# Start stage of a Fourier and attention block: transform tables split earlier, final sums taken before the halves of u, squares of the latent rows asked one block ahead

## The chip, the cores and the metric

The kernel runs on one core of one Trainium2 chip. The metric is device microseconds (us) of one execution. The kernel before takes 1317.43 us, the median of three runs (1315.72 to 1318.75).

## The reference

One mixer layer over 512 latent tokens of width 2048, with 256 context tokens and one conditioning vector `c`. A combined projection of the normalised and modulated rows feeds attention (branch A) and a two-dimensional Fourier mix (branch B); both are gated, projected, merged and projected once more.

```python
shift, scale, gate = jnp.split(silu_c @ w_ada[l] + b_ada[l], 3, axis=-1)
h = _modulate(_rmsnorm(xs, norm_g[l]), shift[:, None], scale[:, None])
p = h @ w_l
...
y = jnp.fft.fftn(ug, axes=(1, 3), norm="ortho").real      # u, the columns u_b of p
...
y_b = (_fourier_mix(u_b) * jax.nn.silu(z_b)) @ w_pb       # z, the columns z_b of p
```

Everything is float32. The kernel multiplies it as three products of split numbers: each operand is written as a high part (rounded) and a low part (what is left), and high·high, low·high and high·low are summed.

## The kernel before, in words

Only the start stage, about the first 180 us, is touched by the change. The rest is eight groups of a Strassen-like scheme for the other columns of the projection, attention, the two branch projections and the output; its instructions stay in the same order on TensorE.

**Rows and tiles.** `xt` holds the 16 blocks of 128 latent channels ("rows" 0 to 15, 512 tokens each). The start stage computes eight tiles of 128 columns: t = 0 to 3 are u, t = 4 to 7 are z. It goes over the row blocks (`kb`) in order; `some(n)` issues the next n tiles of `start_work`, three matmuls each (L329 high·high, L330 with the low part of the row, L331 with the low part of the weights). The four sums of u stay in four PSUM banks (`pb`). The sums of z go through two banks (`pc`) and are added to `part` in SBUF by `keep` (L636 a copy on ACT; L640 an add on DVE; L638 the last add, with the correction `corr`).

**Two forms of a row.** The norm factor `rx` needs the squares of all 16 rows. So rows 0 to 4 (`RAWS` = 5) are multiplied as gain·x without it (`make_raw`, L611 and L612) and their sums are multiplied by `rx` later (`spread_rows`, L737). Rows from 5 on are made with it (`make_h`, L619 to L621; L620 on ACT makes the high part, L621 on DVE the low part). `squares` (L526 on ACT, L528 on DVE) adds up the squares of one chunk of `xt` as it comes; `norm_sum` (L591 to L595) sums them over partitions on TensorE, with square root and reciprocal; `norm_spread` (L600, L601) brings the factor to all partitions.

**Modulation.** `modulate(k)` (L542) is a matrix-vector product of `c` with 2 MB of `w_ada` for row block k, loaded as two transfers into four buffers; ACT copies its sum (L551), TensorE turns it (L555) and DVE makes gain and shift (L561 to L564) in `columns(k)`. Row k can be made only after that.

**Weights.** Pieces of 512 KB or less are loaded into `raw` buffers (L214) and split: ACT makes the high part (L178), DVE the low part (L179). In the first blocks SP issues the loads; from block 5 on ACT issues them (`asks[0] = nc.scalar`, `ask_more`), and from the end of the start stage SP again. From block 8 on two more raw buffers are lent (`MORE_RAW`).

**The Fourier mix.** After the last tiles, the two tables over positions (`fsq`, two pieces of 512 KB) and the table over channels (`fch`) are split, `halves(g)` forms the sum and the difference of the two halves of u's tile g (L817, L818) and splits them (`uh`, `ul`), `channels(g)` multiplies by `fch`, `positions(g)` by `fsq`, and `gate_b` (L864, L865) applies the gate of z. Then group 0 begins with the products named `x`; its weights are the pieces `R`, split as `wlo<-R`.

**What sets the order.** TensorE's order is the order of the code (a hand-written schedule). On DVE and ACT a scheduler orders the instructions; `behind(ins)` ties the instructions in its block behind the given ones. Each engine then runs its instructions strictly in order, so an instruction that waits holds all behind it.

Of the kernel before, what the change touches and what calls it, by code (L numbers as in the profile page):

```python
# [18 lines left out]
P = 128  # L19
D = 2048  # L20
T = 512
# [19 lines left out]
MORE_RAW = 8  # L41
# [80 lines left out]
def block_kernel(ctx, tc, xT, ctx_rows, ctx_toks, x, c_row, w_ss, w_gate, vecs, qkg, rope, dft_c, dft_s,  # L122
# [335 lines left out]
    mr, mrp = region("mr")  # L458
# [51 lines left out]
    csum = pap.tile([P, 256], F32, name="csum")  # L510
    sf = pap.tile([P, RAWS, 32], F32, name="sf")
    nc.vector.memset(sf, 0.0)
    corr = ppool.tile([P, NS], F32, name="corr")
    rx = pap.tile([P, T], F32, name="rx")
    t = hm_tile([P, 2, T], F32, name=uid("nm"))
    pick, root = t[:, 0, :].rearrange("p (t c) -> p t c", t=4), t[:, 1, :P]
# [6 lines left out]
    def squares(a, n):  # L523
        for q in range(a, a + n):
            v = sq[q // 2][:, q % 2, :]
            nc.scalar.activation(v, xt[:, q, :], ACT.Square)  # L526
            if q:
                nc.vector.tensor_tensor(total, total, v, op=ALU.add)  # L528

# [102 lines left out]

    def keep(t, acc, kb, nk):
# [3 lines left out]
        elif kb + nk == KK:  # L637
            nc.vector.scalar_tensor_tensor(dst, acc, corr[:, t : t + 1], dst, op0=ALU.add, op1=ALU.add)  # L638
# [43 lines left out]

    def split_next():
        split_piece(next(e for e in ahead if e.out is None and e.kind != "raw"))
# [7 lines left out]
    with tc.manual_schedule(engines={mybir.EngineType.PE}):  # L692
# [10 lines left out]
        for kb in range(RAWS):  # L703
# [29 lines left out]
        ask_more(act, 2)  # L733
# [6 lines left out]
        with behind(ins):  # L740
            spread_rows(4, 5)
            split_next()
        wada[7] = wada_load(7)
        some(2)
        modulate(6)
        some(2)
        with behind((columns(6),)):
            spread_rows(6, 7)
        some(1)
# [3 lines left out]
        some(2)  # L753
        ask_more(ins[1], 2)

        for kb in range(6, KK, 2):
            ins = make_h(kb), make_h(kb + 1)
            ins = ins[0] + ins[1]
            if kb == MORE_RAW:
# [1196 lines left out]
```

## Time and profile before

| quantity | value |
|---|---|
| median of three runs | 1317.43 us (1315.72 to 1318.75) |
| the profiled execution | 1318.22 us, its span 1316.4 us, 0.79 us above the median |
| mean granted TensorE clock | 0.992 |
| TensorE busy | 1282.3 us, 97% of the span |
| DVE busy | 1010.2 us, 77% |
| ACT busy | 691.7 us, 53% |
| data moved | 318.54 MB, 242 GB/s in the mean |

A row of the timeline reads: start, duration, engine, line, operation, tile written <- tiles read, shape, count, and in brackets the idle time of the engine just before it with what ended that idle time. "ACTq" is an issue of a transfer on ACT's queue. A row of the windows view reads: stretch, then busy us and number of instructions of TensorE (PE), its weight loads (PEld), DVE, ACT and POOL, then the granted TensorE clock (1.00 is full speed), the share of the DMA engines and GB/s. A row of the waits view reads: engine, tile, line, the thing waited for: us in total, times, longest.

### The profile page before, as it was taken

Reading aid. Unit: us, or ns where it says so; the run is one execution under the profiler, and the core shown is the slowest. Engines: PE = TensorE matmul, PEld = TensorE weight load, DVE = VectorE, ACT = ScalarE, POOL = GpSimd, SP = SyncE. Lnnn points to the kernel's source line nnn. Section 1 sums busy time; section 2 is a strip of 40 time slices with the busy share of each in tenths; the row PEclk is TensorE's granted clock in tenths of the full one; section 3 lists DMA queues with packets and bytes.
Section 4 is the critical chain, followed back from the end, with each engine's and each line's share of the span. In section 5 each row is a group of like instructions: output and inputs, shape, how many; then the busy total and the mean of one; then the engine's idle time right before and its main releaser. Section 6 shows DMA issues by size and latency. Waiting matters only on the chain.

```text
span 1316.4 us, 17688 instructions
## 1 busy us (share of the span) xinstructions
PE 1282.3 (97%) x6568; PEld 1051.8 (80%) x6568; DVE 1010.2 (77%) x1326; ACT 691.7 (53%) x1095; POOL 176.2 (13%) x236
## 2 busy tenths in 40 slices
PE   8899899999999999999999999999999999999997
PEld 5566698888888788888888888788888888888885
DVE  4677889978788688666677756688888867887676
ACT  4433555555545455434345454666667645565544
POOL 0011011020112101011012020011210212221210
PEclk9899999999999999999999999999999999999998
DMA  9899558798799989986969898658872899998985
GB/s 381 327 347 380 189 160 205 233 210 286 201 248 267 253 295 280 290 227 172 263 208 254 297 230 249 211 193 249 257 231 88 221 247 243 252 211 225 225 205 171
DMA packets 103862, 318.54 MB, mean 242 GB/s; under 512 B 9824, under 2 KB 33120, under 8 KB 99680
## 3 DMA queue, kind: packets, MB, share of 16 engines
q0 software_dynamic: 29136, 115.36, 38.0%
q1 hardware_dynamic: 50016, 172.56, 36.9%
q10 hardware_dynamic: 24624, 29.50, 6.5%
q8 instruction: 51, 0.84, 0.3%
q14 instruction: 35, 0.29, 0.1%
HBM read 283.30 MB, written 34.09 MB: 241 GB/s over the span
## 4 chain that ended last, share of the span: by engine, by line
PE 78%; DMA 6%; DVE 6%; ACT 2%; issue 2%; ACTq 0%; DVEq 0%
PE banks L329 10%; PE banks L330 10%; PE banks L331 10%; PE x L331 7%; PE x L330 7%; PE x L329 7%; PE y L330 6%; PE y L329 6%; PE y L331 6%; PE banks L1444 2%; DMA wr<-in_w_g 2%; DVE wlo L179 2%; DMA wr<-in_ctx_toks 1%; PE pd L542 1%; DMA wa<-in_w_ss 1%
## 5 line engine op out<-in xcount | busy, mean ns | idle before, releaser
L178 ACT ACTIVATE whi<-R 128x1024 fp32r<-128x1024 f32 x138 | 145.2, 1059 | 141.9 <-PE banks L331 49.5
L179 DVE TENSOR_TENSOR wlo<-R,whi 128x1024 fp32r<-128x1024 f32 x138 | 167.5, 1221 | 55.5 <-ACT whi L178 55.3
L179 DVE TENSOR_TENSOR wlo<-wr,whi 128x1024 fp32r<-128x1024 f32 (+2 forms) x124 | 148.3, 1204 | 66.0 <-ACT whi L178 65.9
L178 ACT ACTIVATE whi<-wr 128x1024 fp32r<-128x1024 f32 (+2 forms) x124 | 128.8, 1044 | 128.4 <-PE y L331 37.4
L329 PE MATMUL banks<-whi,s 128*128 128x512 f32 x396 | 157.0, 396 | 2.1 <-DVE ev L1012 1.5
L330 PE MATMUL banks<-wlo,s 128*128 128x512 f32 x396 | 155.2, 392 | 0.0
L331 PE MATMUL banks<-whi,s 128*128 128x512 f32 x396 | 155.2, 392 | 0.0
L329 PE MATMUL x<-whi,s 128*128 128x512 f32 x352 | 137.2, 390 | 0.0
L331 PE MATMUL x<-whi,s 128*128 128x512 f32 x352 | 137.0, 389 | 0.0
L330 PE MATMUL x<-wlo,s 128*128 128x512 f32 x352 | 136.9, 389 | 0.0
L330 PE MATMUL y<-wlo,s 128*128 128x512 f32 x316 | 123.1, 389 | 1.9 <-DVE wlo L179 1.9
L329 PE MATMUL y<-whi,s 128*128 128x512 f32 x316 | 123.1, 389 | 0.6 <-DVE cxe L1165 0.6
L331 PE MATMUL y<-whi,s 128*128 128x512 f32 x316 | 122.8, 389 | 0.0
L282 POOL DMA_DIRECT2D R<-in_w_g x64 | 56.0, 877 | 421.4 <-DVE wlo L179 246.7
L178 ACT ACTIVATE s<-wr 128x512 fp32r<-128x512 f32 (+2 forms) x93 | 60.5, 676 | 65.0 <-DMA wr<-cf_d 22.3
L179 DVE TENSOR_TENSOR s<-wr,s 128x512 fp32r<-128x512 f32 (+2 forms) x93 | 67.0, 749 | 32.3 <-ACT s L178 31.6
L329 PEld LDWEIGHTS banks<-whi,s 128*128 128x128 f32 x396 | 74.4, 188 | 17.6 <-ACT whi L178 1.9
L331 PEld LDWEIGHTS banks<-whi,s 128*128 128x128 f32 x396 | 74.4, 188 | 15.4
L330 PEld LDWEIGHTS banks<-wlo,s 128*128 128x128 f32 x396 | 74.5, 188 | 14.3 <-DVE wlo L179 0.4
L331 PEld LDWEIGHTS x<-whi,s 128*128 128x128 f32 x352 | 66.1, 188 | 13.8
L329 PEld LDWEIGHTS x<-whi,s 128*128 128x128 f32 x352 | 66.1, 188 | 13.7
L330 PEld LDWEIGHTS x<-wlo,s 128*128 128x128 f32 x352 | 66.1, 188 | 13.6
(305 smaller groups left out, 2860.0 us busy)
## 6 DMA issues: line engine op xcount, KB each, us to landing
wr<-in_w_g SPq DMA_DIRECT2D x128, 512.0 KB, 5.3
R<-in_w_g POOLq DMA_DIRECT2D x64, 512.0 KB, 7.7
wa<-in_w_ss POOLq DMA_DIRECT2D x18, 1024.0 KB, 8.0
R<-in_w_g SPq DMA_DIRECT2D x32, 512.0 KB, 5.7
wr<-in_w_gate SPq DMA_DIRECT2D x32, 512.0 KB, 5.1
wa<-in_w_ss SPq DMA_DIRECT2D x14, 1024.0 KB, 13.4
wr<-in_w_o SPq DMA_DIRECT2D x24, 512.0 KB, 7.7
R<-in_w_o POOLq DMA_DIRECT2D x24, 512.0 KB, 8.7
```

The costliest lines, as they stand in the source:

```text
L178: first = nc.scalar.activation(hi, src, ACT.Copy)
L179: return first, nc.vector.tensor_tensor(lo, src, hi.bitcast(F32), op=ALU.subtract)
L282: nc.gpsimd.dma_start(chain[e.pc], e.nxt, accum_op=ALU.add)
L329: nc.tensor.matmul(o, ah, bh, start=start, stop=False, skip_group_check=cont)
L330: nc.tensor.matmul(o, ah, bl, start=False, stop=False, skip_group_check=cont)
L331: nc.tensor.matmul(o, al, bh, start=False, stop=stop, skip_group_check=cont)
L542: nc.tensor.matmul(acc[32 * j : 32 * j + 32], c2[:, n, :], w[:, k, :], start=n < 4, stop=n >= KK - 4)
L1444: nc.tensor.transpose(tp[:, k * P : (k + 1) * P], p[:, k * P : (k + 1) * P], ident)
```

## The change

1. The first table over positions and the table over channels are loaded one piece earlier and split inside block 10; the second table is split after the start stage. `fsq` becomes two tiles. `fch` and the first `fsq` lie in a pool that lives longer.
2. The two extra raw buffers are gone; instead a raw buffer counts as free as soon as its piece is split.
3. The halves of u are tied behind z's last keeps: halves 0 and 1 behind the keep of tile 4, halves 2 and 3 behind that of tile 5. The weights of group 0 are split one by one behind z's last keep and the positions of each group.
4. The squares of a chunk are asked one block earlier (chunks 1 and 2 in block 0, then one chunk each), and the last chunk's are asked ahead of the split and the row of block 4. The norm's sum moves behind the sums of shifts and the mat-vec of block 4, its spreading one tile later, and the mat-vec for row 6 into block 4.
5. Two loads of weights at the end of block 4 are issued by SP, where ACT issued them.
6. In block 10 the mat-vecs of rows 12 and 13 no longer follow each other directly.

The core of the diff:

```diff
     for p in start_pieces():
-        if p[2:5:2] == (KK - 4, 4):
-            for q in range(2):
-                stream(("dfts", q), dft_s[:, q], 1024, 2, "raw")
+        if p[2:5:2] == (KK - 4, 0):
+            stream(("dfts", 0), dft_s[:, 0], 1024, 2, "raw")
             stream(("dftc", 0), dft_c, 256, 1, "raw")
+        elif p[2:5:2] == (KK - 4, 4):
+            stream(("dfts", 1), dft_s[:, 1], 1024, 2, "raw")
...
     def split_next():
-        split_piece(next(e for e in ahead if e.out is None and e.kind != "raw"))
+        e = next(e for e in ahead if e.out is None and e.kind != "raw")
+        split_piece(e)
+        if e.key[1][2] >= RAWS:
+            e.raws = []
...
             some(5 if kb == 0 else 2)
+            shift_sums(kb)
+            copied = modulate(kb + 1)
             if kb == RAWS - 1:
                 norm_sum()
-            shift_sums(kb)
-            copied = modulate(kb + 1)
             some(1 if kb == 0 else 2)
-            with behind((copied, columns(kb + 1))):
+            last = columns(kb + 1)
+            if kb + 2 == RAWS:
+                with behind((copied,)):
+                    copied = squares(*XCH[RAWS])
+            with behind((copied, last)):
                 if kb:
                     split_next()
             if kb + 1 < RAWS:
-                ins = make_raw(kb + 1)
+                with behind((copied,)):
+                    ins = make_raw(kb + 1)
                 some(2 if kb == 0 else 4)
                 with behind(ins):
-                    squares(*XCH[kb + 1])
-                    if kb + 2 == RAWS:
-                        squares(*XCH[RAWS])
+                    for i in ((1, 2), (3,), (4,), ())[kb]:
+                        squares(*XCH[i])
             else:
-                some(1)
-                act = norm_spread()
-                some(3)
-            if kb + 2 <= RAWS:
+                some(2)
+                norm_spread()
+                modulate(6)
+                some(2)
+            for _ in range(1 if kb + 2 <= RAWS else 2):
                 load_start()
         shift_columns()
         asks[0] = nc.scalar
-        ask_more(act, 2)
...
+            elif kb == 10:
+                some(4)
+                modulate(12)
+                some(2)
+                columns(12)
+                some(2)
+                modulate(13)
+                some(1)
+                columns(13)
+                some(1)
+                with behind(ins):
+                    split_table(0)
+                    split_from(get(("dftc", 0)), fch[:, 0, :], fch[:, 1, :])
             else:
                 some(8 if kb == 8 else 4)
                 modulate(kb + 2)
...
-    for q in range(2):
-        split_from(get(("dfts", q)).rearrange("p (m n) -> p m n", m=2), fsq[:, 0, q], fsq[:, 1, q])
-    raw = get(("dftc", 0))
-    split_from(raw, fch[:, 0, :], fch[:, 1, :])
-    for g in range(4):
-        halves(g)
     ordered = ExitStack()
     ordered.enter_context(tc.manual_schedule(engines={mybir.EngineType.PE}))
+    for n in range(4):
+        next(work)
+        if n < 2:
+            with behind((finals[-1],)):
+                halves(2 * n)
+                halves(2 * n + 1)
     for _ in work:
         pass
...
         positions(g)
         if g < 2:
             channels(g + 2)
+        with behind((finals[-1],)):
+            for e in ahead[:g]:
+                split_piece(e)
     ordered.close()
+    look[0] = 4
```

Line numbers in the rows of the change are those of the changed kernel: most start-stage lines stand one to three lines off (L178 is its split on DVE, L177 on ACT, L328 to L330 its three products, L641 its last keep, L643 its keep).

**ACT, from block 3 to block 4.** `ado` is the copy of a mat-vec's sum, `L526` the squares, `whi_513` (in the change `whi_523`) the high part of block 4's weights, `s_517` (`s_527`) the high part of row 4. Before:

```order
33 L551 COPY ado_496<-pd_159 128x256
34 L611 ACTIVATE s_517<-xt,gain 128x512
35 L566 COPY sf<-shift 128x1
36 L178 ACTIVATE whi_513<-wr_460 128x1024
37 L526 ACTIVATE s_156<-xt 128x512 x2
38 L526 ACTIVATE s_157<-xt 128x512 x2
39 L526 ACTIVATE s_158<-xt 128x512 x2
40 L636 COPY part<-pb_224 128x512
```

Now:

```order
33 L552 COPY ado_500<-pd_157 128x256
34 L526 ACTIVATE s_154<-xt 128x512 x2
35 L526 ACTIVATE s_155<-xt 128x512
36 L567 COPY sf<-shift 128x1
37 L526 ACTIVATE s_155<-xt 128x512
38 L526 ACTIVATE s_156<-xt 128x512 x2
39 L177 ACTIVATE whi_523<-wr_464 128x1024
40 L612 ACTIVATE s_527<-xt,gain 128x512
```

The last six squares stood behind row 4 and the split of block 4's weights; now they stand ahead of both.

**TensorE, block 4.** `pb` and `pc` are the first two tiles of block 4, L591 (L592) the norm's sum over partitions, L575 (L576) the sums of shifts, L542 (L543) the mat-vec for row 5. Before:

```order
122 L329 MATMUL pc_559<-s_517,whi_513 128x512
123 L330 MATMUL pc_559<-s_518,whi_513 128x512
124 L331 MATMUL pc_559<-s_517,wlo_514 128x512
125 L591 MATMUL pc_564<-s_151,ones 128x512
126 L575 MATMUL pd_159<-wr_460,sf 32x256 x4
127 L542 MATMUL pd_160<-wa_463,c_131 32x256 x8
128 L542 MATMUL pd_160<-wa_465,c_131 32x256 x8
```

Now:

```order
122 L328 MATMUL pc_557<-s_527,whi_523 128x512
123 L329 MATMUL pc_557<-s_528,whi_523 128x512
124 L330 MATMUL pc_557<-s_527,wlo_524 128x512
125 L576 MATMUL pd_157<-wr_464,sf 32x256 x4
126 L543 MATMUL pd_158<-wa_467,c_128 32x256 x8
127 L543 MATMUL pd_158<-wa_469,c_128 32x256 x8
128 L592 MATMUL pc_585<-s_149,ones 128x512
```

The norm's sum has moved behind twenty small matmuls.

**DVE, the end of the start stage.** `u`, `ul` are halves of u and their low parts, `part<-pc` z's last keeps. Before, ahead of these rows, stand the splits of both `fsq` pieces and of `fch`:

```order
194 L817 TENSOR_TENSOR u_1366<-part 128x256
195 L818 TENSOR_TENSOR u_1366<-part 128x256
196 L817 TENSOR_TENSOR u_1371<-part 128x256
197 L818 TENSOR_TENSOR u_1371<-part 128x256
198 L179 TENSOR_TENSOR wlo_1391<-R_1343,whi_1390 128x1024
199 L179 TENSOR_TENSOR ul<-u_1366,uh 128x512
200 L179 TENSOR_TENSOR ul<-u_1371,uh 128x512
201 L817 TENSOR_TENSOR u_1376<-part 128x256
202 L818 TENSOR_TENSOR u_1376<-part 128x256
203 L817 TENSOR_TENSOR u_1381<-part 128x256
204 L818 TENSOR_TENSOR u_1381<-part 128x256
205 L638 SCALAR_TENSOR_TENSOR part<-pc_1394,corr,part 128x512
```

Now:

```order
192 L641 SCALAR_TENSOR_TENSOR part<-pb_225,corr,part 128x512
193 L178 TENSOR_TENSOR fsq_1353<-wr_1161,fsq_1353 128x1024
194 L641 SCALAR_TENSOR_TENSOR part<-pc_1366,corr,part 128x512
195 L837 TENSOR_TENSOR u_1380<-part 128x256
196 L838 TENSOR_TENSOR u_1380<-part 128x256
197 L837 TENSOR_TENSOR u_1385<-part 128x256
198 L838 TENSOR_TENSOR u_1385<-part 128x256
199 L641 SCALAR_TENSOR_TENSOR part<-pc_1390,corr,part 128x512
```

z's first last keep stood behind three tables, all halves of u and a split of `R`; now it stands behind one table.

More of the change, by code (lines that the diff above doesn't have):

```diff
@@ L38 @@
 NS = len(START)
-MORE_RAW = 8
 RAWS = 5
@@ L513, in block_kernel @@
     corr = ppool.tile([P, NS], F32, name="corr")
+    fch = ppool.tile([P, 2, 256], F32R, name="fch")
+    fsq = [ppool.tile([P, 2, 2, T], F32R, name="fsq0")]
     rx = pap.tile([P, T], F32, name="rx")
     t = hm_tile([P, 2, T], F32, name=uid("nm"))
-    pick, root = t[:, 0, :].rearrange("p (t c) -> p t c", t=4), t[:, 1, :P]
+    pick, root, csum = t[:, 0, :].rearrange("p (t c) -> p t c", t=4), t[:, 1, :P], t[:, 1, 256:]
     nc.gpsimd.memset(pick, 0.0)
@@ L752, in block_kernel @@
         columns(7)
-        some(2)
-        ask_more(ins[1], 2)
+        some(3)
         for kb in range(6, KK, 2):
@@ L810, in block_kernel @@
     ul = fnp.tile([P, 4, T], F32R, name="ul")
-    fch = fnp.tile([P, 2, 256], F32R, name="fch")
-    fsq = fnp.tile([P, 2, 2, 2, T], F32R, name="fsq")
+    fsq.append(fnp.tile([P, 2, 2, T], F32R, name="fsq1"))
+    split_table(1)
     def halves(g):
```

25 lines of the change are left out of this document (11 added, 14 removed).

## The prediction

> **What bounds the kernel now.** First the share of busy time: TensorE works 97% of the span, so what can be won is what TensorE waits, and what it does at half its clock. The waits view lists TensorE's waits over the whole span; these are the four that the change can reach:
>
> ```profile
> PE pc L329 <- DVE part L638: 4.9, 1, 4.9
> PE pc L591 <- DVE s L528: 4.6, 1, 4.6
> PE pd L542 <- DMA wa<-in_w_ss: 2.7, 2, 1.8
> PE pb L329 <- ACT s L620: 1.8, 1, 1.8
> ```
>
> All lie in the first 160 us. The windows view shows where, and where the granted clock falls:
>
> ```profile
> 50.00:60.00 10.00, 4.91 (x27) 1.98 (x30) 6.27 (x10) 4.37 (x10) 0.00 (x0) 0.66 0.61 250
> 70.00:80.00 10.00, 10.00 (x86) 5.84 (x86) 5.88 (x12) 2.43 (x4) 2.16 (x4) 0.83 0.86 316
> 110.00:120.00 10.00, 8.37 (x72) 5.43 (x70) 8.81 (x17) 3.90 (x6) 1.62 (x3) 1.00 0.98 382
> 150.00:160.00 10.00, 5.08 (x17) 3.78 (x16) 10.00 (x18) 6.14 (x9) 0.00 (x0) 0.83 0.79 304
> 190.00:200.00 10.00, 10.00 (x46) 8.28 (x45) 10.00 (x13) 5.68 (x6) 3.41 (x4) 1.00 1.01 200
> ```
>
> In all but the last of these TensorE lacks time or clock; after 160 us it is full. I call the four places A (50 to 60), B (69 to 75), D (118 to 121) and E (150 to 160), and go through them on the axis of the profiled execution.
>
> **A, the norm's sum.** TensorE's timeline at A, then the same two small products one block earlier, at full clock; DVE's adds of squares; on ACT the copy of a mat-vec's sum in block 1 and in block 3, and the squares of block 3:
>
> ```profile
> 56.41 2.08 PE L591 MATMUL pc<-s,ones 128*128 128x512 f32 x2 [4.57 <-DVE s L528]
> 58.41 1.08 PE L575 MATMUL pd<-wr,sf 128*32 128x256 f32 x8
> 59.27 2.17 PE L542 MATMUL pd<-wa,c 128*32 128x256 f32 x32
> ```
> ```profile
> 42.44 0.64 PE L575 MATMUL pd<-wr,sf 128*32 128x256 f32 x8
> 42.90 1.91 PE L542 MATMUL pd<-wa,c 128*32 128x256 f32 x32
> ```
> ```profile
> 52.49 3.87 DVE L528 TENSOR_TENSOR s<-s,s 128x512 f32<-128x512 f32 x5
> ```
> ```profile
> 26.57 0.37 ACT L551 COPY ado<-pd 128x256 f32<-128x256 f32 x1 [2.78 <-PE pd L542]
> 44.93 0.38 ACT L551 COPY ado<-pd 128x256 f32<-128x256 f32 x1 [3.36 <-PE pd L542]
> 49.24 3.22 ACT L526 ACTIVATE s<-xt 128x512 f32<-128x512 f32 x6
> ```
>
> Before, two tiles of block 4 run, begun some 2.4 us before the wait, at 49.4; then the sum waits 4.57 us for five adds (3.87). The change removes that wait, but puts the six squares (3.22) ahead of the split and the row of block 4, and their adds too. So the first tile of block 4 now waits. Two steps fix its start. First, in block 1 the copy of the mat-vec's sum, at 26.57, falls behind squares of a chunk that has not landed yet; that chunk is issued at 10.55 and such loads take 16.2 in the median:
>
> ```profile
> 10.55 0.42 SPq L467 DMA_DIRECT2D xt<-in_xT  x1
> 27.25 0.33 SPq L467 DMA_DIRECT2D xt<-in_xT  x1
> ```
> ```profile
> xt<-in_xT SPq DMA_DIRECT2D x4, 768.0 KB, 16.2
> ```
>
> It lands near 27, its three squares take 3 x 0.54 (a sixth of 3.22 each), and the copy ends near 29.2; TensorE needs it one tile and a half after the mat-vec, near 27.9, so I charge about 1.0 us, once: in block 3 the chunk issued at 27.25 lands near 43.5, before the copy at 44.93. Second, in block 4 DVE has from about 47.4 three keeps and six adds at 0.6, small ones of 0.5, then the low weights 1.2 and the low row 0.65: it ends near 55.2. TensorE has run out near 50.3 (its old 49.4 plus 1.0), does one product in between and stands until 55.2. Then two tiles less one product (five at about 0.43 in the low clock, as in E's rows below), the sums of shifts and the mat-vec (2.2 to 3.2 together) and the norm's sum (1.0 to 2.1): near 61.2, where the mat-vec ended at 61.4 before (59.27 + 2.17). Nearly five us are still waited, at another place. **A is worth 0.2 us**, between -1.5 and +1.5.
>
> **B, the first row made with the norm.** TensorE, then ACT:
>
> ```profile
> 68.93 0.49 PE L329 MATMUL pb<-s,whi 128*128 128x512 f32 x1 [1.82 <-ACT s L620]
> 69.72 0.53 PE L330 MATMUL pb<-s,whi 128*128 128x512 f32 x1 [0.29 <-DVE s L621]
> 71.88 2.69 PE L542 MATMUL pd<-wa,c 128*32 128x256 f32 x32
> ```
> ```profile
> 64.88 2.27 ACTq L214 DMA_DIRECT2D wr<-in_w_start  x1
> 68.16 0.72 ACT L620 ACTIVATE s<-xt,shift 128x512 fp32r<-128x512 f32 x1 [0.30 <-issue]
> ```
>
> ACT's first issue of a load takes 2.27 us in front of the row; TensorE waits 1.82 and 0.29, and runs five matmuls at 0.43 for 0.23 (1.0) and the mat-vec in 2.69 for 1.91 (0.8) until 74.5 (71.88 + 2.69). Sum 3.9. The change lets SP issue that load and the next, and puts the mat-vec for row 6 (1.9) between the norm's spreading and the row, so the chain of factor, row and its low part is hidden by two tiles and a mat-vec. What is late next is row 6: its low part now stands on DVE behind the keep of the tile before last of block 5; I estimate a wait of 0.3 to 1.5, take 0.8, and set 0.2 against it for a small wait at row 7 that was there before. SP has nothing queued behind the two loads but the loads of group 0. **B is worth 3.3 us**, between 1.5 and 4.2.
>
> On the clock a rule speaks against part of this sum. After A's 4.57 and E's 4.92 us of waiting the clock halves; at B it halves after 1.82 and 0.29 with one product between, and at D below it does not after 1.81. The Trainium skill, in "TensorE: Matmul & The Clock Gate", Part 1, has the clock fall to half only after an idle window of some 3.4 us. By that rule B would be 2.1 us of waiting without the 1.8 at low clock, and new waits of 1 us would cost no clock either; the trace agrees at A, D and E and not at B, and the sum keeps the 1.8 that its rows show.
>
> **D, the second mat-vec in block 10.**
>
> ```profile
> 120.17 1.07 PE L542 MATMUL pd<-wa,c 128*32 128x256 f32 x16 [1.81 <-DMA wa<-in_w_ss]
> 121.17 0.50 PE L329 MATMUL pb<-s,whi 128*128 128x512 f32 x1
> ```
> ```profile
> 123.15 0.39 DVE L561 TENSOR_REDUCE adr<-pd 128x4 f32<-128x16 f32 x2 [4.34 <-PE pd L555]
> ```
>
> Between the mat-vecs of rows 12 and 13 now stand four tiles (4 x 0.69 us = 2.8) that ran after them before. They cover the 1.81. But TensorE arrives earlier by A and B, the DMA engines are 0.98 busy there, and a table is loaded ahead of the weights of the last piece; part of the wait can come back at row 15. **D is worth 1.4 us**, between -0.5 and 1.8. The two table splits put into block 10 cost DVE 1.2 + 0.4; DVE is idle 4.34 there while it waits for the gains, and the splits stand after the rows. Without that cover the 1.6 would delay row 12. The two raw buffers that go leave the last weights issued when the block before is split, some 10 us before use; a load takes 4 to 9 us, so I cost them at nothing.
>
> **E, z's last keeps.** TensorE, then DVE:
>
> ```profile
> 155.64 0.77 PE L329 MATMUL pc<-s,whi 128*128 128x512 f32 x1 [4.92 <-DVE part L638]
> 156.20 0.63 PE L330 MATMUL pc<-s,whi 128*128 128x512 f32 x1
> 158.76 0.42 PE L330 MATMUL pc<-s,whi 128*128 128x512 f32 x1
> ```
> ```profile
> 147.12 2.35 DVE L179 TENSOR_TENSOR fsq<-wr,fsq 128x1024 fp32r<-128x1024 f32 x2
> 149.39 0.42 DVE L179 TENSOR_TENSOR fch<-wr,fch 128x256 fp32r<-128x256 f32 x1
> 151.06 1.22 DVE L179 TENSOR_TENSOR wlo<-R,whi 128x1024 fp32r<-128x1024 f32 x1
> 154.75 0.75 DVE L638 SCALAR_TENSOR_TENSOR part<-pc,corr,part 128x512 f32<-128x512 f32 x1
> ```
>
> Tile 6 needs the bank of tile 4. TensorE ran out at 150.7 (155.64 - 4.92) with tile 5, which takes 12 x 0.23, so tile 4's sum was complete at 148; but its keep runs at 154.75, behind 7.6 us of tables, halves and splits. In the change one split (1.2) stands ahead of it: 147.1 + 1.2 + 0.75 gives 149.0, before TensorE ends tile 5 at 150.7. The next keep has four halves (4 x 0.34) before it and is done by 151.5; tile 7 starts at 153.5. So 4.92 goes, and the seven matmuls at 0.43 for 0.23 (156.20 to 158.76, 1.4); the rows of the Fourier mix behind follow closer by another 0.6 since the tables are done. What is late next is DVE:
>
> ```profile
> 180.37 0.69 DVE L858 SCALAR_TENSOR_TENSOR part<-pb,part 128x512 f32<-128x512 f32 x1 [2.19 <-PE pb L331]
> 185.52 1.22 DVE L179 TENSOR_TENSOR wlo<-R,whi 128x1024 fp32r<-128x1024 f32 x1
> ```
> ```profile
> 180.17 0.40 PE L329 MATMUL x<-whi,s 128*128 128x512 f32 x1
> 188.36 0.39 PE L329 MATMUL x<-whi,s 128*128 128x512 f32 x1
> ```
>
> The split that ends at 186.7 is used at 188.6, a margin of 1.9. From 147 to 180 DVE works some 29 us of 33; two splits (1.6) leave that stretch and its waits on TensorE (4.2) shrink, which together is 5.8 of the 6.9 us that it must be quicker; the rest comes out of splits for group 0 that the change puts later, behind the products they are not needed for. The margin then stays near 2 or more. **E is worth 6.9 us**; if DVE is short, down to 3.
>
> **The sum**: 0.2 + 3.3 + 1.4 + 6.9 = 11.8. The profiled execution, 1318.22, would come to 1306.4; it stands 0.79 above the median of 1317.43, so the median comes to **1305.6**.
>
> **The rivals.**
> - *A is worse than moved.* If squares on ACT make TensorE late in more blocks than block 1, or the first tile of block 4 starts at 57, A is -2.5 and the low clock lasts: 1308.5. For it: ACT runs in order, and every load that is late there now stands ahead of a row. Against it: by the rows above the chunk of block 3 lands before the copy.
> - *DVE takes over E.* DVE is 10.00 busy in the window from 190 on, with 1.9 us of margin. If TensorE comes 7 us earlier and DVE cannot follow, group 0 waits and E gives 3: 1309.5. Against it: fewer splits and DVE's waits.
> - *Short waits cool the clock.* As at B, each of the new waits (block 1, row 6, a rest at row 15) could bring five matmuls and a mat-vec at half clock, 1.8 each: 3.6 to 5.4 more, 1310. By the skill's rule above it is nothing.
> - *The slower side: squares hold every block.* If each chunk's squares hold ACT's copy in all four blocks, each costs the 1.1 of block 1 and a low clock of 2.4 (the 4.8 us from 69.7 to 74.5, halved): 14; with A at -1 and the other three at their value the kernel is 14 + 1 - 11.6 = 3.4 us slower, 1320.8. It decides at the landing of the chunk: it would have to land after the mat-vec in all four blocks, and by the loads' 16.2 it does so in the first.
> - *The change does not do what it says*: the keep of tile 4 could wait for something else. In the order it has only one table split before it, so this gets little.
>
> **How the numbers follow.** Forecast as summed (1303.5 to 1307.5): 0.55. Worse A: 0.12. DVE takes over: 0.12. Clock: 0.08. Two or more of these together, near 1314 to 1317: 0.06. Slower: 0.03. Better than summed, as B at 4.2 and A at 1.5: 0.04. The range 1301.5 to 1311.5 leaves out the joint cases and the slower one, and the edges of others. About 0.2%, 2.6 us, is what a measurement of this kernel can tell from no change: faster by more than that 0.92, within it 0.04, slower 0.04.
>
> **What would show it.** A: the wait of 4.57 before L592 is gone and one of 4 to 5 us stands in front of block 4's first L329; the mat-vec for row 5 still ends near 61. B: no wait and clock 1.00 between 66 and 76, and the mat-vec of row 8 some 3.5 us earlier. D: no wait of TensorE on a mat-vec's load over 1 us. E: tile 6 starts with no wait, and the products `x` of group 0 start near 168.4 for 180.17. The prediction is wrong if `x` starts as said and the end does not follow, which would mean a wait on DVE or on a load in group 0.

## The result, and the profile after

The changed kernel takes 1317.72 us in the median of 12 runs (1315.26 to 1318.64), the kernel before 1317.20 in 12 runs beside them (1315.22 to 1320.79). The ratio is 1.0001, with a 95% interval of 0.9992 to 1.0011: no change, where 11.8 us less was forecast. The profiled execution has a span of 1316.8 us and a mean granted clock of 0.991 (before 1316.4 and 0.992).

The waits view of the change; lines stand as in the changed kernel:

```profile
PE pd L543 <- DMA wa<-in_w_ss: 6.8, 3, 3.5
PE pb L328 <- ACT s L612: 3.7, 2, 3.5
PE pb L329 <- DVE s L613: 2.3, 4, 1.0
PE pd L556 <- ACT ado L552: 1.7, 2, 1.2
PE y L329 <- DVE s L178: 1.2, 1, 1.2
```

The 4.9 on `part`, the 4.6 on the norm's sum and the 1.8 on row 5 have gone. The wait for mat-vec loads has grown from 2.7 to 6.8, and 3.5 on row 4 is new. The windows, at the stretches shown before and two more:

```profile
50.00:60.00 10.00, 5.47 (x24) 2.97 (x26) 6.89 (x12) 3.91 (x7) 0.00 (x0) 0.67 0.86 352
70.00:80.00 10.00, 9.57 (x67) 6.47 (x66) 9.96 (x21) 3.40 (x8) 1.08 (x2) 1.00 0.93 359
110.00:120.00 10.00, 10.00 (x89) 6.50 (x91) 9.19 (x20) 3.94 (x7) 1.09 (x3) 1.00 0.92 329
130.00:140.00 10.00, 5.45 (x43) 3.19 (x43) 0.00 (x0) 0.38 (x1) 0.00 (x0) 0.66 0.37 149
150.00:160.00 10.00, 10.00 (x45) 8.27 (x45) 9.58 (x19) 7.09 (x9) 0.00 (x0) 1.00 1.01 404
230.00:240.00 10.00, 8.35 (x29) 6.11 (x28) 9.16 (x10) 4.33 (x7) 1.44 (x2) 0.83 0.70 179
```

D and E are full now (110 to 120, 150 to 160) and B nearly so (9.57 from 70 to 80, clock 1.00). A has hardly moved. Two holes are new: 130 to 140, with TensorE at 5.45 and the clock at 0.66, and 230 to 240. For the first, the same stretch of before:

```profile
130.00:140.00 10.00, 10.00 (x95) 7.27 (x95) 6.33 (x18) 3.42 (x6) 0.00 (x0) 1.00 0.35 118
```

95 matmuls ran there, 43 do now. As a ledger: the start of the same TensorE instruction in both timelines, and what each stretch gave.

| up to | before | after | after minus before | gain of the stretch | forecast |
|---|---|---|---|---|---|
| first tile behind row 5's mat-vec and the norm's sum (A) | 61.37 | 62.41 | +1.04 | −1.0 | 0.2 |
| mat-vec of row 12 (B) | 115.57 | 113.52 | −2.05 | 3.1 | 3.3 |
| mat-vec of row 14 (D) | 130.02 | 126.36 | −3.66 | 1.6 | 1.4 |
| first `pc` tile behind row 15's mat-vec | 136.94 | 141.41 | +4.47 | **−8.1** | 0 |
| second product with `fsq` (E) | 165.90 | 163.44 | −2.46 | 6.9 | 6.9 |
| first `x` of group 0 | 180.17 | 177.50 | −2.67 | 0.2 | |
| end of the waits in group 0 | 235.05 | 238.20 | +3.15 | **−5.8** | 0 |
| product `y` at 444 | 443.99 | 444.93 | +0.94 | 2.2 | |
| last matmul | 1306.60 | 1306.98 | +0.38 | 0.6 | |

The four sources gave 10.6 of 11.8. Two places that the sum had at nothing took 13.9 back; 3.0 came behind them, most of it because a wait of 1.93 that before has at 443.66 is absent now.

**The first loss** on TensorE's timeline of the change, block 12, and the mat-vecs of rows 14 and 15 in before:

```profile
126.36 1.93 PE L543 MATMUL pd<-wa,c 128*32 128x256 f32 x32
131.06 1.10 PE L543 MATMUL pd<-wa,c 128*32 128x256 f32 x16 [2.76 <-DMA wa<-in_w_ss]
135.65 1.94 PE L543 MATMUL pd<-wa,c 128*32 128x256 f32 x16 [3.48 <-DMA wa<-in_w_ss]
```
```profile
130.02 3.66 PE L542 MATMUL pd<-wa,c 128*32 128x256 f32 x64
```

In before both run without a wait. In the change each half of row 15's mat-vec waits for its own transfer; they land at 130.93 and 135.61, where the last landed at 130.94 before. The two waits are 6.24, and the second half takes 1.94 where the first took 1.10: the clock is at half, which with the tiles behind it makes up most of the rest of 8.1. Three of the four loads of `w_ada` for rows 14 and 15 were issued earlier than before (all between 114.9 and 120.9, for 117.0 to 121.6; the third 1.3 later), and all four landed later. Issues between 110 and 130, before and after (issue and tile, count, KB each, median us to landing):

```profile
wa<-in_w_ss POOLq DMA_DIRECT2D x4, 1024.0 KB, 8.3
wr<-in_w_start ACTq DMA_DIRECT2D x2, 512.0 KB, 5.2
wr<-in_dft_s ACTq DMA_DIRECT2D x1, 512.0 KB, 9.3
```
```profile
wa<-in_w_ss POOLq DMA_DIRECT2D x4, 1024.0 KB, 11.2
wr<-in_w_start ACTq DMA_DIRECT2D x3, 512.0 KB, 9.4
wr<-in_dft_s ACTq DMA_DIRECT2D x1, 512.0 KB, 10.2
```

What runs beside them is seen on ACT's queue of the change:

```profile
112.62 1.47 ACTq L213 DMA_DIRECT2D wr<-in_w_start  x2
117.16 0.33 ACTq L213 DMA_DIRECT2D wr<-in_dft_s  x1
118.29 0.98 ACTq L213 DMA_DIRECT2D wr<-in_w_start  x1
```

These are 1.75 MB within 6 us, just ahead of and between the four loads of 1 MB; from 110 to 119 before issues 0.6 MB (512 KB at 110.31, 128 KB at 114.69).

**The second loss.** TensorE, DVE and ACT of the change in group 0, and DVE of before:

```profile
190.26 0.50 PE L330 MATMUL y<-whi,s 128*128 128x512 f32 x1 [0.63 <-DVE s L178]
231.22 0.39 PE L328 MATMUL y<-s,s 128*128 128x512 f32 x1
232.78 0.50 PE L329 MATMUL y<-s,s 128*128 128x512 f32 x1 [1.18 <-DVE s L178]
233.12 0.40 PE L328 MATMUL x<-s,s 128*128 128x512 f32 x1
```
```profile
187.84 1.23 DVE L178 TENSOR_TENSOR wlo<-R,whi 128x1024 fp32r<-128x1024 f32 x1 [3.82 <-ACT whi L177]
188.98 2.35 DVE L178 TENSOR_TENSOR s<-Z,s 128x1024 fp32r<-128x1024 f32 x2
```
```profile
186.75 1.06 ACT L177 ACTIVATE whi<-R 128x1024 fp32r<-128x1024 f32 x1 [5.24 <-PE x L330]
```
```profile
180.98 2.35 DVE L179 TENSOR_TENSOR s<-Z,s 128x1024 fp32r<-128x1024 f32 x2
```

In the change ACT stands 5.24 us in front of a split of R until TensorE has read an older weight out; DVE stands 3.82 us behind it, and the splits of Z wait behind both until 188.98. In before they ran at 180.98. DVE then is full and stays late until 232, where the clock falls too (0.83).

The 5.8 falls into two parts. By 231.65 of before 2.0 are lost, with the waits around 190. The other 3.8 are lost in the next 3.4 us, and there the order on TensorE is not that of before, although the code of group 0 was not edited: the two products `y` at 231.22 and 232.78 now stand ahead of twelve products `x`, behind which before has them:

```profile
234.60 0.39 PE L329 MATMUL y<-s,s 128*128 128x512 f32 x1
```

So the statement further up that TensorE's order behind the start stage stays the same doesn't hold here. Every version below that builds on the changed kernel with both tables has the two products moved, and loses 1.6 to 3.8 there; the versions with the old order lose less than 0.1 there. Which part of the change moved them, no run separates.

### The profile page after: what moved, and what is told of

Its sections match the earlier page's. It is cut to its first block, busy times and chain, and to the rows that moved or that the text cites. A ratio compares the mean times of both kernels' runs of the same rounds, so it can differ in the third digit from the quotient of the medians.

```text
span 1316.8 us, 17681 instructions
## 1 busy us (share of the span) xinstructions
PE 1283.5 (97%) x6568; PEld 1051.9 (80%) x6568; DVE 1008.6 (77%) x1326; ACT 690.3 (52%) x1095; POOL 175.9 (13%) x236
## 4 chain that ended last, share of the span: by engine, by line
PE 84%; DVE 7%; DMA 4%; issue 2%; ACT 2%; SPq 0%; ACTq 0%; POOL 0%; DVEq 0%; POOLq 0%
PE banks L328 10%; PE banks L329 10%; PE banks L330 10%; PE x L330 8%; PE x L329 8%; PE x L328 8%; PE y L330 7%; PE y L328 7%; PE y L329 7%; PE banks L1468 2%; DMA xt<-in_xT 2%; DVE wlo L178 2%; PE pd L543 1%; DMA wa<-in_w_ss 1%; PE pb L329 1%
## 5 line engine op out<-in xcount | busy, mean ns | idle before, releaser
L177 ACT ACTIVATE whi<-R 128x1024 fp32r<-128x1024 f32 x138 | 145.1, 1058 | 140.5 <-PE banks L330 51.5
L178 DVE TENSOR_TENSOR wlo<-R,whi 128x1024 fp32r<-128x1024 f32 x138 | 167.3, 1220 | 58.5 <-ACT whi L177 58.4
L178 DVE TENSOR_TENSOR wlo<-wr,whi 128x1024 fp32r<-128x1024 f32 (+2 forms) x124 | 148.3, 1203 | 63.6 <-ACT whi L177 63.4
L177 ACT ACTIVATE whi<-wr 128x1024 fp32r<-128x1024 f32 (+2 forms) x124 | 128.5, 1044 | 117.1 <-PE y L330 35.9
L328 PE MATMUL banks<-whi,s 128*128 128x512 f32 x396 | 156.9, 396 | 1.9 <-DVE ev L1036 1.5
L330 PE MATMUL banks<-whi,s 128*128 128x512 f32 x396 | 155.1, 392 | 0.0
L328 PE MATMUL x<-whi,s 128*128 128x512 f32 x352 | 137.2, 390 | 0.0
L330 PE MATMUL x<-whi,s 128*128 128x512 f32 x352 | 137.0, 389 | 0.0
L328 PE MATMUL y<-whi,s 128*128 128x512 f32 x316 | 123.2, 390 | 1.0 <-DVE cxe L1189 0.8
L330 PE MATMUL y<-whi,s 128*128 128x512 f32 x316 | 122.9, 389 | 0.6 <-DVE s L178 0.6
L177 ACT ACTIVATE s<-wr 128x512 fp32r<-128x512 f32 (+2 forms) x93 | 60.4, 676 | 76.8 <-DMA wr<-in_w_g 22.1
L178 DVE TENSOR_TENSOR s<-wr,s 128x512 fp32r<-128x512 f32 (+2 forms) x93 | 66.7, 748 | 33.7 <-ACT s L177 32.9
L328 PEld LDWEIGHTS banks<-whi,s 128*128 128x128 f32 x396 | 74.4, 188 | 17.1 <-ACT whi L177 1.9
L330 PEld LDWEIGHTS banks<-whi,s 128*128 128x128 f32 x396 | 74.4, 188 | 15.5
L328 PEld LDWEIGHTS x<-whi,s 128*128 128x128 f32 x352 | 66.1, 188 | 13.7
L330 PEld LDWEIGHTS x<-whi,s 128*128 128x128 f32 x352 | 66.1, 188 | 13.7
L329 PEld LDWEIGHTS x<-wlo,s 128*128 128x128 f32 x352 | 66.1, 188 | 13.6
```

The source lines that it names most:

```text
L177: first = nc.scalar.activation(hi, src, ACT.Copy)
L178: return first, nc.vector.tensor_tensor(lo, src, hi.bitcast(F32), op=ALU.subtract)
L328: nc.tensor.matmul(o, ah, bh, start=start, stop=False, skip_group_check=cont)
L329: nc.tensor.matmul(o, ah, bl, start=False, stop=False, skip_group_check=cont)
L330: nc.tensor.matmul(o, al, bh, start=False, stop=stop, skip_group_check=cont)
```

## The experiments

All ratios are to the kernel before, run beside them, with the 95% interval; 0.001 is 1.3 us. Of each edit only the core is shown. Two theories stood for the first loss. *The buffers*: four raw buffers where there were six move the loads later, into the time of the mat-vec loads (part 2, with the earlier tables of part 1). *The order*: with tiles between the mat-vecs of block 10 (part 6) the loads of rows 14 and 15 are issued at another time. For group 0: the order of splits at the end of the stage (part 3), or DVE short of time in any case.

**The halves of u alone.** The kernel before, with part 3's tie only:

```diff
-    for g in range(4):
-        halves(g)
+    for n in range(4):
+        next(work)
+        if n < 2:
+            with behind((finals[-1],)):
+                halves(2 * n)
+                halves(2 * n + 1)
```

> The kernel before, with one part of the change alone: the halves of u are tied behind z's last keeps (tables, loads, squares and block 10 as before). Theory 1 (the gain at E is real, and the change loses it again at two places that are not part of E: late mat-vec loads in block 12 because the ring of raw buffers went from six to four, and group 0, whose splits of Z stand behind a split of weights that must wait for a buffer): TensorE's wait of 4.92 at tile 6 shrinks to about 1, products x of group 0 start 5.5 to 6.5 us earlier, no new wait in group 0 because the splits of Z stand ahead of that split as before; 1311.5 us, 5 to 6.5 below before. Rival (DVE is the bound from 190 on and takes over whatever E gives): waits of TensorE on DVE's splits in group 0 sum to 4 or more and the time is within 2 us of before.

Ratio 0.9954 (0.9936 to 0.9972), about 6 us. The wait of 4.9 at tile 6 has shrunk to this:

```profile
PE pc L329 <- DVE part L640: 1.0, 1, 1.0
```

Group 0 loses 1.3 here, not 5.8, though the tie is the same. So E's gain is the tie of the halves, and the larger part of group 0's loss isn't its price. D's wait is there as before, behind one of 0.42, and this time the clock falls with it (0.83 from 120 to 130, for 1.00 before):

```profile
120.44 1.50 PE L542 MATMUL pd<-wa,c 128*32 128x256 f32 x16 [2.11 <-DMA wa<-in_w_ss]
```

**The squares alone.** The kernel before with parts 4 and 5: squares one block ahead, norm's sum moved, mat-vec of row 6 in block 4, two loads by SP.

```diff
+            if kb + 2 == RAWS:
+                with behind((copied,)):
+                    copied = squares(*XCH[RAWS])
...
-                    squares(*XCH[kb + 1])
+                    for i in ((1, 2), (3,), (4,), ())[kb]:
+                        squares(*XCH[i])
```

> The kernel before, with the squares one block ahead, the norm's sum and the mat-vec of row 6 moved, and the two loads by SP (parts 4 and 5 of the change); tables, six raw buffers, block 10 and the end of the stage as before. Theory 1 (ring of buffers): the 2 to 3 us won by block 8 stay, no wait above 1 us on a mat-vec load behind block 10 beyond the 1.8 of before; 1314 to 1315.5 us. Rival (the transfers up to 130 us are the bound, whatever the order): TensorE arrives earlier at the mat-vecs of rows 13 to 15 and waits there for what it won, 1317 us.

Ratio 0.9975 (0.9961 to 0.9989). Block 4 waits 3.5 and 1.3, E's wait is back at 5.0, and block 12 has no wait. By the times parts 4 and 5 give about 3.3 (1.4 to 5.1), where A and B had 3.5 together in the forecast and 2.1 in the ledger. The profiled execution doesn't show the gain: its first `x` starts 1.9 later than that of before. The first loss is not theirs.

**Block 10 in its old order.** The changed kernel without part 6:

```diff
-                modulate(12)
-                some(2)
-                columns(12)
-                some(2)
-                modulate(13)
-                some(1)
+                modulate(12)
+                modulate(13)
+                some(2)
+                columns(12)
                 columns(13)
-                some(1)
+                some(4)
```

> The changed kernel with block 10's mat-vecs of rows 12 and 13 back to back as before (part 6 undone), all else as changed. Rival theory (part 6 frees the buffers of row 13 late, so the loads for row 15 are issued late): the waits of 2.76 and 3.48 on the loads of rows 14 and 15 go to below 2 in sum and the time falls to about 1312. Theory 1 (ring of four buffers, loads of weights issued beside those of the mat-vecs): the waits in block 12 stay above 4 in sum, and the 1.8 at row 13 may return; 1316.5 to 1319.

Ratio 1.0001 (0.9984 to 1.0018). TensorE in block 12:

```profile
135.87 1.51 PE L543 MATMUL pd<-wa,c 128*32 128x256 f32 x12 [3.94 <-DMA wa<-in_w_ss]
```

The first wait is 1.80 instead of 2.76, the second is longer. The order theory fell. The run shows one thing more: with the old order the mat-vecs of rows 12 and 13 run without a wait too.

```profile
114.65 3.66 PE L543 MATMUL pd<-wa,c 128*32 128x256 f32 x64
```

**All but the tables and the buffers.** The kernel before with parts 3, 4, 5 and 6; tables, six raw buffers and the splits of group 0 as in before.

> The kernel before, with parts 3 (halves only), 4, 5 and 6 of the change, but tables, their loads and six raw buffers as before. Theory 1: gains of e1 and e2 and 1 to 1.4 us at row 13 add up, no wait over 2 us in block 12: 1307 to 1310. If transfers bound the stage: waits for mat-vec loads in blocks 10 to 12 eat what parts 4 and 5 won, 1311 to 1312. If DVE bounds group 0: 1315 or more.

Ratio 0.9931 (0.9914 to 0.9949), about 9 us. The mat-vecs wait:

```profile
PE pd L543 <- DMA wa<-in_w_ss: 0.5, 2, 0.3
```

The 6.8 is down to 0.5, and group 0 loses 1.3. So both losses come with parts 1 and 2 and the later splits of group 0. The gains of the first two runs add up (0.0046 and 0.0025, here 0.0069 with part 6 as well; the intervals leave room for D's 1.4).

**Four buffers or six.** Both are the changed kernel with the first table neither loaded nor split, the second used in its place, so the Fourier mix is computed with one table twice. The first keeps four raw buffers, the second lends two from block 8 on:

```diff
+            if kb == 8:
+                raw_pools.insert(0, (mrp, 2, "raw", 2))
```

> The changed kernel without the first table over positions: it is neither loaded nor split, and the second table is used in its place (so the Fourier mix is computed with the wrong half of the table). Four raw buffers as in the change. It frees 8 KB for the twin of this run. Theory 1 (the ring of four buffers holds back the loads of weights, so that they are issued beside the mat-vec loads of rows 14 and 15): although 512 KB less is moved, TensorE still waits 3 us or more for the loads of rows 14 and 15, and the bytes moved from 90 to 110 us stay below 360 GB/s. Rival (the table's load and split ahead of the last weights are the cause): the waits are below 1.5.

> As the run with four raw buffers and without the first table, but with the two extra raw buffers from block 8 on, as the kernel before has them. Theory 1: the loads of weights are issued before 100 us again, 90 to 110 us moves 370 GB/s or more, the waits for rows 14 and 15 are below 1.5 in sum, and the time is 4 to 7 us below its twin. Rival: no difference to its twin beyond 1.5 us.

Ratios 0.9958 (0.9943 to 0.9973) and 0.9940 (0.9918 to 0.9962). With four buffers and with six:

```profile
133.70 1.94 PE L542 MATMUL pd<-wa,c 128*32 128x256 f32 x16 [3.85 <-DMA wa<-in_w_ss]
```
```profile
PE pd L543 <- DMA wa<-in_w_ss: 2.8, 2, 1.5
```

The waits for rows 14 and 15 are 4.0 with four buffers and 2.8 with six, and more was moved earlier: 419 and 343 GB/s in the two windows from 90 to 110, for 369 and 320. In the profiles the second is 3.4 us ahead at 146. But 4 to 7 us were expected, the medians differ by 0.8 with overlapping intervals, and the waits of one set of loads vary by more than 1.2 from one execution to the next (below). So it isn't shown that the buffers matter; it is shown that 2.8 stays with six. In both runs the order in group 0 is that of before.

**One ask less in block 10.** The changed kernel, with the loads at the end of block 10 asked a block later.

```diff
-            ask_more(ins[1], 8)
+            if kb != 10:
+                ask_more(ins[1], 8)
```

> The changed kernel with the second ask for loads in block 10 left out, so that the second table and the next piece of weights are asked in block 12, behind row 12, and no longer stand in the queues ahead of the mat-vec loads of row 15. Theory 1 (1 MB beside the mat-vec loads): the waits for rows 14 and 15 shrink from 6.2 to 2 to 4 us, the time falls by 2 to 4 us to about 1314. Rival (the mat-vec buffers come free too late): the waits stay within 1 us of 6.2.

Ratio 1.0004 (0.9995 to 1.0014). The issues moved by only 1.5 us (to 118.72 and 120.05), and 4.7 us of waits stayed: the edit hardly did what it was for, and tells little.

**The same loads, behind the mat-vec.** The changed kernel, four raw buffers, all tables; the second table and the last two pieces of weights are asked when row 14's mat-vec is copied out:

```diff
-            ask_more(ins[1], 8)
+            if kb != 12:
+                ask_more(ins[1], 8)
...
-                modulate(kb + 2)
+                copied = modulate(kb + 2)
+                if kb == 12:
+                    ask_more(copied, 8)
...
-            ask_more(ins[1], 8)
+            if kb != 10:
+                ask_more(ins[1], 8)
```

> The changed kernel with the loads of the second table and of the last two pieces of weights asked only behind the copy of row 14's mat-vec (1.5 MB moved from 117 to 126 us to about 128 us). The run with the second ask of block 10 left out moved them by 1.5 us only, so it tested little. Theory 1 (loads queued beside those of rows 14 and 15 make them late): the waits for rows 14 and 15 fall from 6.2 to below 2, tile t=4 of the last block is reached 5 us earlier than in the changed kernel; 1311 to 1314. Rival (too few bytes moved before 110 us is enough to make them late, whatever is queued later): waits of 4 or more stay.

Ratio 0.9937 (0.9913 to 0.9960), about 8 us. ACT's queue, TensorE, the issues from 110 to 130, and two windows:

```profile
129.52 0.33 ACTq L213 DMA_DIRECT2D wr<-in_dft_s  x1
129.88 0.46 ACTq L213 DMA_DIRECT2D wr<-in_w_start  x1
```
```profile
130.57 1.07 PE L543 MATMUL pd<-wa,c 128*32 128x256 f32 x16 [0.33 <-DMA wa<-in_w_ss]
```
```profile
wa<-in_w_ss POOLq DMA_DIRECT2D x4, 1024.0 KB, 7.8
```
```profile
100.00:110.00 10.00, 10.00 (x95) 6.95 (x94) 7.83 (x19) 2.74 (x5) 2.15 (x4) 1.00 0.83 279
130.00:140.00 10.00, 9.67 (x63) 7.39 (x56) 5.32 (x14) 3.72 (x5) 0.00 (x0) 1.00 0.57 207
```

The loads for rows 14 and 15 land after 7.8 instead of 11.2, the waits are 0.5 in all, and the clock stays at 1.00. That is one execution. The last version of the next part asks its loads just as late, and in its profile TensorE still waits 2.29 for the last of the four, with the clock at 0.83 from 130 to 140. Where the loads are asked as in the change, the waits are 6.2 in the change and 6.6 and 5.0 in the two tries on group 0. So late loads took away 2.7 us of waiting at least, but not always all of it. The run has four buffers, and fewer bytes moved from 100 to 110 (279 GB/s) than in the change (313) and in before (360). So neither the ring nor the bytes left over cost the time by themselves: it is the 512 KB loads that ACT issues from 117 on (at 117, 118 and 126), which reach the DMA engines beside loads that TensorE needs first.

**Group 0, two tries.** The changed kernel with Z asked two pieces earlier, and then with the splits of group 0's weights left to the looking ahead that before has:

```diff
-    return [(f, pc % 2, ready)] if f and g == 0 and (pc > 1 or name == "P2") else []
+    return [(f, pc % 2, ready)] if f and g == 0 and (pc < 2 if name == "P1" else pc > 1 or name == "P2") else []
```
```diff
-    may[0], asks[0] = 1 << 30, nc.sync
+    may[0], asks[0], look[0] = 1 << 30, nc.sync, 4
...
-        with behind((finals[-1],)):
-            for e in ahead[:g]:
-                split_piece(e)
-    look[0] = 4
```

> The changed kernel with the splits of the two Z forms asked two pieces earlier in group 0, so that they stand on ACT and DVE ahead of the weights split that waits for a buffer. Theory 1b (group 0's loss is order: ACT and DVE idle from 183 to 188 behind that split while Z waits): DVE's idle 3.8 before the split is filled, TensorE's waits on DVE's splits of Z at 189 to 190 (0.9) and those at 231 to 234 (1.7 with half clock after) go; 4 to 5 us below the changed kernel, 1313. Rival (DVE has simply too much work from 150 to 235): the waits at 231 stay above 1 us and the gain is below 1.5.

> The changed kernel with the weights of group 0 split by looking ahead from the end of the start stage on, as before, and not one by one behind z's last keep. Theory 1b' (those splits, put behind the Fourier mix's rows, push the adds to R and with them the loads of the next weights late): the adds to R run 5 to 10 us earlier, group 0 loses below 2 us in place of 5.7, and the time is 2 to 4 us below the changed kernel. Rival (order of Z alone): group 0's waits at 189 and 231 stay within 1 us.

Ratios 1.0002 (0.9990 to 1.0013) and 0.9998 (0.9981 to 1.0015). With Z earlier the loss between the first `x` and 238 is 3.0 instead of 5.8, so the place of Z's splits is part of it: 1.3 are lost by 231.65 and 1.6 at the moved products `y`, for 2.0 and 3.8. The time doesn't follow, and why not is open. With the splits left to looking ahead the loss is 4.9 and the waits at 231 stand (1.19 and 0.47): that they are written out later is not the cause. Both keep the waits in block 12. Z earlier was also put on the version with late loads:

> The late loads of the run before together with the splits of Z two pieces earlier. If the two losses (mat-vec loads, group 0) are separate, their repairs add: waits for rows 14 and 15 below 2 and group 0's loss near 3 in place of 5.7; 1309 to 1312. If group 0 only takes what block 12 gives, no better than the late loads alone.

Ratio 0.9935 (0.9914 to 0.9956), against 0.9937 without: nothing that can be told apart.

**What the runs point to.** The version with all but the tables and buffers, but the squares behind the row as in before; only the norm's sum is moved, behind the first four tiles of block 4, and the mat-vec of row 6 ahead of its spreading:

```diff
-            if kb == RAWS - 1:
-                norm_sum()
...
-            if kb + 2 == RAWS:
-                with behind((copied,)):
-                    copied = squares(*XCH[RAWS])
...
-                with behind((copied,)):
-                    ins = make_raw(kb + 1)
+                ins = make_raw(kb + 1)
                 some(2 if kb == 0 else 4)
                 with behind(ins):
-                    for i in ((1, 2), (3,), (4,), ())[kb]:
-                        squares(*XCH[i])
+                    squares(*XCH[kb + 1])
+                    if kb + 2 == RAWS:
+                        squares(*XCH[RAWS])
             else:
+                norm_sum()
                 some(2)
-                norm_spread()
                 modulate(6)
+                norm_spread()
```

> The best so far (halves tied behind the keeps, block 10 reordered, loads by SP, tables and six raw buffers as before) with the squares asked in the order of before and only the norm's sum moved: behind the first four tiles of block 4. Theory 2 (A's wait does not move but goes, if the squares stay behind the rows): the waits of 1.0 in block 1 and 4.5 in block 4 vanish, TensorE reaches block 6 some 4 to 5 us earlier; if the loads of weights keep up, 1306 to 1308. Rival (transfers bound 60 to 130 us): new waits for weights or mat-vec loads in blocks 6 to 12 take it, 1310 to 1312.

1304.61 us, ratio 0.9889 (0.9865 to 0.9913), about 14.6 us less than before and faster than both kernels; its mean clock is 0.998. TensorE, and the window of A:

```profile
56.16 1.13 PE L592 MATMUL pc<-s,ones 128*128 128x512 f32 x2 [0.60 <-DVE s L528]
```
```profile
50.00:60.00 10.00, 9.13 (x88) 5.51 (x92) 8.89 (x16) 6.87 (x14) 1.26 (x2) 1.00 1.02 417
```

The norm's sum waits 0.60 for the same adds for which it waited 4.57, since four tiles stand in front of it; 88 matmuls run in the stretch, where before had 27 and the change 24. At the start of row 8's mat-vec it is 8.1 us ahead of before (79.11 for 87.22), the change 2.1.

## Why the prediction was wrong

**The step that failed** is the last of D: "The two raw buffers that go leave the last weights issued when the block before is split, some 10 us before use; a load takes 4 to 9 us, so I cost them at nothing." The cost is 8.1 us. The second table and the last two pieces also took longer than 4 to 9 us: 10.2, 13.6 and 9.4. The sentence asked only whether the weights come in time for their own use, and they do: no wait of TensorE in the change is put down to them. It left out what they do to the others: with late loads kept away the four loads of 1 MB land after 7.8, with them after 11.2. I had the parts of this in hand: "a table is loaded ahead of the weights of the last piece; part of the wait can come back at row 15". I bounded it by D's own 1.81 instead of by rows. In before the last of the four loads lands at 130.94 and is needed after three quarters of the 3.66 us from 130.02 on, at 132.8: a slack of 1.8. The change issues 1.1 MB more beside them (1.75 for 0.63), at the 404 GB/s of the window from 120 to 130 an estimated 2.9 us, which is the difference of the medians (11.2 and 8.3); the last lands 4.7 later. TensorE comes 3.7 earlier. 4.7 + 3.7 - 1.8 is 6.6, and 6.24 was waited. The half clock comes on top.

**A** (0.2 forecast, −1.0 measured) is right within its bounds. The forecast's mechanism held: the wait of 4.57 is now one on row 4's parts.

```profile
54.64 0.80 PE L328 MATMUL pb<-s,whi 128*128 128x512 f32 x1 [3.50 <-ACT s L612]
56.46 0.79 PE L329 MATMUL pb<-s,whi 128*128 128x512 f32 x1 [1.02 <-DVE s L613]
29.17 0.44 PE L556 MATMUL pd<-ident,ado 128*128 128x128 f32 x2 [1.21 <-ACT ado L552]
```

4.52 stand for 4.57 and the copy in block 1 costs 1.21 for the 1.0 charged; block 3 adds waits of 0.23 and 0.67 where before has one of 0.53, and ends 1.77 late. Row 4's low part comes at 56.4, where the sum had 55.2.

**B** (3.3; 3.1) and **E** (6.9; 6.9) are right in size, and the traces show the cause: the waits are gone. The run of the halves shows E alone; that of the squares has A and B together. ACT's 2.27 us at B are not the price of a first issue, though: its first in the change, at 69.17, takes 0.39.

**D** (1.4; 1.6) is right in size, but partly by luck. The forecast had four tiles cover the wait, with row 13's last load as late as before. In the change that load lands 10.2 after its issue at 104.71, at 114.9; in before it took 13.35 from 106.78 on and landed at 120.1. So without part 6 there is no wait either, as block 10 in its old order shows. Fewer other loads stood beside it (313 GB/s from 100 to 110, for 360). That these are the bytes that came back beside rows 14 and 15 is argued, not shown.

**Group 0** (0 forecast, −5.8 measured). The step that failed is "The margin then stays near 2 or more", at E. "DVE takes over E" was a rival with 0.12 and 3.9 lost; its reason, DVE short of time, is only half right. In the window from 180 DVE has time left, which it spends behind the split of R:

```profile
180.00:190.00 10.00, 9.38 (x40) 7.13 (x38) 4.96 (x5) 4.31 (x5) 0.63 (x1) 1.00 0.80 302
```

4.96 busy, where I expected a margin; then it is full from 190 on and can't make it up. That the order of splits set it is shown in part (Z earlier: 3.0). By 231.65 that version has lost the 1.3 of the versions with the old end of the stage; the rest stands at the two products `y` that moved ahead on TensorE. The prediction reckoned with no change of order there, and what caused it stays open. The sign that the prediction named for being wrong, `x` near 168.4 and an end that does not follow, isn't what came: `x` starts at 177.5, since most of the gain was already lost in block 12.

The joint case had 0.06 and ended at 1317. It held what happened, but the two losses were taken as independent mishaps with small prices.

## What to carry to other kernels

When a change moves loads, cost them twice: whether they land in time for their own use, and whose transfers they land beside. Set the bytes that are issued within the flight time of a critical load against the rate of that window, and ask how much slack the consumer has after all the other gains have brought it forward. A load with slack is best asked after the one without; here two loads of 512 KB asked some 12 us later, and one 4 us later, were worth about 8 us. And a wait for a sum that nothing needs soon is best covered by putting independent work in front of it on the waiting engine; making its inputs earlier only moved the wait. Last, compare the order of instructions behind the edited stage as well: here it had changed unasked, 50 us behind it.

## What the runs showed of the hardware

The granted clock after short waits is not fixed by their length. At one place of group 0 waits of 1.18 and 0.47 brought the window to 0.83 in the change, and waits of 1.21 and 0.47 left it at 1.00 with late loads. At row 13's mat-vec a wait of 1.81 left it at 1.00 in before; waits of 0.42 and 2.11 in the halves alone brought it to 0.83:

```profile
120.00:130.00 10.00, 9.56 (x49) 7.11 (x50) 4.43 (x12) 3.28 (x5) 0.54 (x1) 0.83 0.98 398
```

The rule that the prediction weighed, in the Trainium skill, "TensorE: Matmul & The Clock Gate", Part 1, has the clock fall after an idle window of some 3.4 us and the windows run free of the kernel. The free running fits that equal waits end differently; the length does not agree, since the clock fell after waits that come to 1.65 in the change, 2.5 in the halves alone and, with the squares alone, 2.2 (0.53 and 1.69). So waits of one to two us in this kernel may cost their own length or up to 1.7 us more (0.17 of ten), and no row here tells beforehand which.

A transfer that is issued later, on another engine's queue, slows one that is under way: in the change the loads of row 14 were issued at 114.9 and 115.8, ahead of the table at 117.2, and landed at 123.4 and 127.2, the second after 11.4 us; with the table and the weights asked at 129.5 it landed after 8.7. The Trainium skill, "DMA: Bandwidth & Descriptors", "Queues, rings and completion order", says that each DMA engine takes turns between its queue rows, packet by packet; the landings agree with that, and no run here tells the turns themselves from other causes of the delay.
